# Small products run in halves, and the late modulation moved into the second scan and the output projection

## The chip, the core and the metric

The kernel runs on one core of a Trainium2 chip. The time is the device time of one execution in microseconds. Its engines are TensorE (matrix products; PE in the profile, PEld for its weight loads), VectorE (DVE), ScalarE (ACT), GpSimd (POOL) and SyncE (SP), whose queue issues all transfers. Each engine has a fixed list of instructions and runs it in order.

## The reference

One layer of a hybrid diffusion backbone: 512 latent tokens (`x`) and 256 context tokens, width 1024, all in float32.

```python
mod = silu(c) @ w_ada + b_ada                      # six vectors of 1024: sh1 sc1 gt1 sh2 sc2 gt2
h  = rms_norm(x, g_norm1) * (1 + sc1) + sh1        # hc likewise for the context
aq, ak, av, dq, dk, dv, dz, da, db, ga, gd = split_cols(h @ w_in)
y_attn = window_ctx_attention(...)                 # 8 query heads of 64, 2 key heads
o, _, _ = bidir_delta(q, k, v, g, beta, s_cf, s_cb) # gated delta rule, both directions, chunks of 64
y = sigmoid(ga) * (y_attn @ w_br_attn) + sigmoid(gd) * (merge_norm(o, dz) @ w_br_dn)
x1 = x + gt1 * (y @ w_out)
out = x1 + gt2 * (square(relu(modulate(rms_norm(x1, g_norm2), sc2, sh2) @ w_mlp1)) @ w_mlp2)
```

In the delta rule each chunk of 64 tokens and each of 8 heads needs the product of its keys with each other (`kk`), a triangular solve with it, and the product of queries and keys (`intra`). A scan over 4 context chunks and then over 8 latent chunks carries a 64x64 state for each head and direction.

## The kernel before, in words

**Large products.** All weights come in tiles of 128x1024 (512 KB, 256 KB for the branch projections). `wload` loads one into a ring of four slots (`wr`), ScalarE makes a rounded high part of it (L261) and VectorE the rest (L262). `mm3` and `gate_tiles` multiply with three products of 128x128 by 512 for each of eight slices, so a whole tile is 24 large products in one PSUM bank.

**Small products.** `half_products` (L690) makes, for four chunks at a time, the key products (source `kT`) or the query products (source `qT`) in blocks of 32: 128 products of 64x32 by 32, each of which is two matmul instructions in the profile, so 256 a call. It is called three times in `chunk_mats` (L702), once for each group of four chunks, and twice before the second scan (L1173). `combine` (L783) joins the inverses of the two halves of a chunk: a loop of 64 products of 32x32 (L791, L792), a copy of their result by ScalarE (L793), and a second loop of 64 (L800, L801). It is called once in the attention stage and twice between the scans (L1160).

**The order of the work.** The Python code writes the work of several generators in turn. `weave` takes the next piece of the generator that is least far on; the matrices of the delta rule (`mats`, 16 pieces) are woven with the attention inputs (`attn_in`, taken 32 times). `run_fill(n)` puts n large products from a filler (the attention branch projection, then gate tiles) between other work: `FILL[1]` = 28 before each `combine`, `FILL[2]` = 36 before each `half_products` of the queries, and 8, 7, 3 by turns in the three parts of a scan step. From this the framework's scheduler makes each engine's list, and may move pieces that don't depend on each other; TensorE's list was read for the counts below.

**The scan.** `chain_step` (L1037) is one chunk in one direction: products with the state (L1051), VectorE forms the residual (L1055, L1056), products with the inverse (L1063), VectorE scales (L1069) and ScalarE copies, products for the new state (L1082) and the output (L1100), VectorE makes the new state (L1093) and adds the output (L1105 or L1108). `steps` runs the two directions side by side and yields three times a step, 24 times in the eight latent steps.

**The late modulation.** `late_mod` (L999) computes the four modulation vectors that are needed late, in 4 groups of 8 steps: gt1, sh2, sc2, gt2. A step loads 512 KB of `w_ada` into a slot of the same ring `wr` (L1003) and reduces it on VectorE (L1005). `run_late(n)` takes n of the first 24 steps; the last 8 run in the MLP. gt1 is used in `residual` (L1268) by way of L1255, sc2 by way of L1283 (`mA`) and sh2 in the second norm (L277). `LATE` = 6, 3, 0 takes 6 before each `combine`, 3 before each `half_products` of the queries, none in the scan, and the rest behind it (L1201).

**The output projection** (L1275) is five tiles of 24 large products, each followed by `residual`, and three more tiles in halves of the tokens; then the second norm and the MLP.

Of the kernel before, what the change touches and what calls it, by code (L numbers as in the profile page):

```python
# [18 lines left out]
FILL = 144, 28, 36, (8, 7, 3)  # L19
# [6 lines left out]
ADVE = (4, 6)  # L26
ATT = 32
NHALF = 3
LATE = 6, 3, 0
NPL = ()  # L30
WEARLY = 0
ND1 = 3
# [10 lines left out]
HC = CH // 2  # L43
# [53 lines left out]
def tile_layer(ctx: ExitStack, tc: tile.TileContext, I: dict, out: bass.AP, dbg=None):  # L97
# [167 lines left out]
    def mm3(acc, w, xs, start=True, stop=True, ks=None):  # L265
        ks = list(range(len(xs))) if ks is None else ks
        n = len(ks)
        for i, k in enumerate(ks):
            xhi, xlo = xs[i]
            PE.matmul(acc, w[0][:, k, :], xhi, start=(start and i == 0), stop=False)  # L270
            PE.matmul(acc, w[0][:, k, :], xlo, start=False, stop=False)  # L271
            PE.matmul(acc, w[1][:, k, :], xhi, start=False, stop=(stop and i == n - 1))  # L272
# [286 lines left out]
    def weave(*work):  # L559

        done = [0] * len(work)
        while True:
            left = [(d / n, i) for i, (d, (_, n)) in enumerate(zip(done, work)) if d < n]
            if not left:
                break
            i = min(left)[1]
            next(work[i][0], None)
            done[i] += 1
# [65 lines left out]
    kT = [alloc(TOK, True) for _ in range(4)]  # L634
# [55 lines left out]
    def half_products(D_, O_, gi, src):  # L690

        for i in range(16):
            c, q = gi * 4 + i // 4, i % 4
            for x, dst in enumerate((D_, O_)):
                for h in range(2):
                    for a in range(2):
                        r = slice(64 * a, 64 * a + 64)
                        o, o2 = col(c) + HC * h, col(c) + HC * (h ^ x)
                        PE.matmul(dst[quad(a, h), i * HC:(i + 1) * HC], kT[q][r, o:o + HC], src[q][r, o2:o2 + HC],
                                  start=True, stop=True)  # L700

    def chunk_mats(gi):  # L702
        ms = slice(gi * 16, gi * 16 + 16)
        kD, kO = bank(), bank()
        half_products(kD, kO, gi, kT)
        yield
        dO = bank()
        for d in range(2):
            mg, mb = alloc(1024), alloc(512)
            row = lambda m_: m_[:, d, :].unsqueeze(1).broadcast_to([P, 16, HC])  # L710
            G.tensor_tensor(v3(mb.ap), row(nmask), bc(btok[:, d, ms], HC), op=ALU.mult)
            dp = bank()
            for x in range(2):
                gx = mg[:, x * 512:x * 512 + 512]
                V.tensor_tensor(v3(r32(gx)), row(mi), bc(gsp[:, x, d, ms], HC), op=ALU.mult)
                PE.matmul(dp.ap, trr[:, d, :], r32(gx), start=(x == 0), stop=(x == 1))
                PE.matmul(dO.ap, trr[:, 2 + d, :], r32(gx), start=(d == x == 0), stop=(d == x == 1))
            mg.free()
            if gi == 0:
                eb = alloc(512)  # L720
                e, na = eb.ap, neg[0][:, d * 512:d * 512 + 512]
            else:
                o = (gi - 1) * 512
                e, na = ED[d][:, o:o + 512], neg[1 + d][:, o:o + 512]
            act(e, dp.ap, AF.Exp)
            dp.free()
            V.tensor_tensor(e, e, mb.ap, op=ALU.mult)
            mb.free()
            V.tensor_tensor(na, e, kD.ap, op=ALU.mult)
            if gi == 0:  # L730
                eb.free()
            yield
        eb = alloc(512) if gi == 0 else None
        e = eb.ap if gi == 0 else EO[:, (gi - 1) * 512:gi * 512]
        act(e, dO.ap, AF.Exp)
        V.tensor_tensor(v3(e), v3(e), bc(tbO[:, ms], HC), op=ALU.mult)
        V.tensor_tensor(NTO[gi].ap, e, kO.ap, op=ALU.mult)
        for b in (kD, kO, dO, eb):
            if b:
                b.free()  # L740
        yield
# [38 lines left out]

        V.transpose(dst.rearrange("p m i -> p i m"), X3[g].rearrange("p r s -> p s r") if swap else X3[g])

    def combine(nto, XTf, XRf, XTb, XRb, XAf, XAb, inplace):  # L783

        Y, Ys = bank(), alloc(512)
        nt = v3(nto.ap)
        for i in range(16):
            o = slice(i * HC, (i + 1) * HC)
            for a in range(2):
                lo, hi = quad(a, 0), quad(a, 1)  # L790
                PE.matmul(Y[hi, o], nt[lo, i], XRf[lo, i], start=True, stop=True)  # L791
                PE.matmul(Y[lo, o], nt[hi, i], XRb[hi, i], start=True, stop=True)  # L792
        A.activation(Ys.ap, Y.ap, AF.Copy)  # L793
        Y.free()
        XO = bank()
        for i in range(16):
            o = slice(i * HC, (i + 1) * HC)
            for a in range(2):
                lo, hi = quad(a, 0), quad(a, 1)
                PE.matmul(XO[lo, o], Ys[hi, o], XTf[hi, i], start=True, stop=True)  # L800
                PE.matmul(XO[hi, o], Ys[lo, o], XTb[lo, i], start=True, stop=True)  # L801
        Ys.free()
        xo = v3(XO.ap)
        if not inplace:
            A.activation(XAf[:, :, :HC], XTf, AF.Copy)
            A.activation(XAb[:, :, :HC], XTb, AF.Copy)
        for a in range(2):
            lo, hi = quad(a, 0), quad(a, 1)
            A.activation(XAf[hi, :, HC:], XTf[hi], AF.Copy)
            A.activation(XAb[hi, :, HC:], XTb[hi], AF.Copy)  # L810
            A.activation(XAf[lo, :, HC:], xo[lo], AF.Copy)
            A.activation(XAb[hi, :, :HC], xo[hi], AF.Copy)
            G.memset(XAf[hi, :, :HC], 0.0)
            G.memset(XAb[lo, :, HC:], 0.0)
        XO.free()

# [16 lines left out]
    qT = []  # L833
# [8 lines left out]
    def mats():  # L842
        for q in range(4):
            l2n(kT[q].ap, 1.0, ((0, SEQ), (SEQ, TOK)), epsc)
            yield
        for gi in range(3):
            yield from chunk_mats(gi)
# [5 lines left out]
        yield from v_attn()  # L853

    att = attn_in()
    weave((mats(), 16), (att, ATT))
    tri_.free()
    trr_.free()
    lowm = alloc(1024)
# [160 lines left out]
    def run_late(n):  # L1020
        for _ in range(n):
            if late_n[0] < 24:
                late_n[0] += 1
                next(late)

    def run_fill(n):
        for _ in range(n):
            next(fill, None)
# [126 lines left out]
    for g in range(2):  # L1155
        ms = slice(16 * g, 16 * g + 16)
        f, b = xa[0][:, ms], xa[1][:, ms]
        run_fill(FILL[1])
        run_late(LATE[0])
        combine(NTO[1 + g], f[:, :, :HC], xr3[0][:, ms], b[:, :, :HC], xr3[1][:, ms], f, b, True)  # L1160
        NTO[1 + g].free()
    for b in xr:
        b.free()
# [3 lines left out]
    for g in range(2):  # L1167
        ms = slice(16 * g, 16 * g + 16)
        es = slice(512 * g, 512 * g + 512)
        run_fill(FILL[2])  # L1170
        run_late(LATE[1])
        qD, qO = bank(), bank()
        half_products(qD, qO, 1 + g, qT)  # L1173
        for d in range(2):
            V.tensor_tensor(ia[d][:, ms, :HC], v3(ED[d][:, es]), v3(qD.ap), op=ALU.mult)
        V.tensor_tensor(EO[:, es], EO[:, es], qO.ap, op=ALU.mult)
        qD.free()
        qO.free()
        eo = v3(EO[:, es])
        for a in range(2):  # L1180
            lo, hi = quad(a, 0), quad(a, 1)
            for d in range(2):
                A.activation(ia[d][hi, ms, HC:], ia[d][hi, ms, :HC], AF.Copy)
            A.activation(ia[0][lo, ms, HC:], eo[lo], AF.Copy)
            A.activation(ia[1][hi, ms, :HC], eo[hi], AF.Copy)
            G.memset(ia[0][hi, ms, :HC], 0.0)
            G.memset(ia[1][lo, ms, HC:], 0.0)
# [6 lines left out]
    ot = ot_.ap.rearrange("p (c q v) -> p c q v", c=NCL, q=4)  # L1194
    for n, _ in enumerate(steps(range(NCC, NC_))):
        run_fill(FILL[3][n % 3])
        if n % 3 == 2:
            run_late(LATE[2])
    for _ in fill:
        pass  # L1200
    run_late(24)  # L1201
    for b in kT + qT + KTM[1:] + VTM[1:] + XA[1] + IA + zb + Sb[0] + Sb[1]:
        b.free()

# [60 lines left out]
    def residual(ct, acc, cols):  # L1265

        x = xn_[ct][:, cols]
        V.scalar_tensor_tensor(x, acc.ap[:, cols], gt1h[:, ct:ct + 1], x, op0=ALU.mult, op1=ALU.add)  # L1268
        sq = ssq if ct == 0 else alloc(512)
        A.activation(sq[:, cols], x, AF.Square)  # L1270
        if ct:
            V.tensor_tensor(ssq[:, cols], ssq[:, cols], sq[:, cols], op=ALU.add)
            sq.free()

    for ct in range(8 - NHALF):  # L1275
        w = wnext()
        acc = bank()
        mm3(acc.ap, w, ys)
        residual(ct, acc, slice(0, 512))
        acc.free()  # L1280
    rx = alloc(512)
    mA = small([P, 8], "mA2", bufs=1)
    V.scalar_tensor_tensor(mA, modT[:, 2], 1.0, g2, op0=ALU.add, op1=ALU.mult)  # L1283
# [202 lines left out]
```

## Time and profile before

| | us |
|---|---|
| median of 3 runs | 958.29 (957.17 to 960.55) |
| the profiled execution | 959.2 |
| its span, first to last instruction | 957.4 |

| engine | busy, us | share | instructions |
|---|---|---|---|
| TensorE, matmuls | 917.7 | 96% | 7684 |
| TensorE, weight loads | 737.1 | 77% | 7684 |
| VectorE | 597.9 | 62% | 1010 |
| ScalarE | 449.3 | 47% | 827 |

The mean granted clock of TensorE over the span was 0.986. The page cuts the span into 40 slices of 23.9 us; a digit is the busy share in tenths, and PEclk is the granted clock in the same way. A group of instructions is named by its line in the kernel, its engine and its operation. A wait names the engine and line that ended it; "issue" stands for idle time that no other engine or transfer ended. TensorE busy does not mean TensorE at full speed: at a lowered clock it is busy as well. The stages, by the starts of their instructions: delta matrices about 105 to 155 us, first scan to about 372, `combine` and query products 372 to 431, second scan 431 to 512, branch and output projections 520 to 600, MLP to the end.

### The profile page before, as it was taken

How to read it: one execution, taken by the hardware profiler on the slowest of the kernel's cores; microseconds unless marked ns; L12 is line 12 of the kernel's file. 1: busy time of each engine (PE TensorE's matmuls, PEld its weight loads, DVE VectorE, ACT ScalarE, POOL GpSimd, SP SyncE). 2: the span in 40 equal slices, each digit the busy share in tenths (PEclk: the TensorE clock that was granted, in tenths of full speed). 3: DMA queues.
4: the chain of work that ended last, by engine and by line, in shares of the span. 5: the costliest groups of instructions: out<-in, count | busy, mean ns of one | idle time of the engine just before them, and what ended most of it. 6: DMA issues, size and time to landing. Idle time of an engine off the chain costs nothing. (4 is left out here: it accounts for less than half of the span.)

```text
span 957.4 us, 18072 instructions
## 1 busy us (share of the span) xinstructions
PE 917.7 (96%) x7684; PEld 737.1 (77%) x7684; DVE 597.9 (62%) x1010; ACT 449.3 (47%) x827; POOL 36.4 (4%) x45
## 2 busy tenths in 40 slices
PE   7999989989999999869999999999999999999998
PEld 3578767876877677658887889988888888888886
DVE  0876688997788899745567665982365225423511
ACT  6456745337667887337555433561154115313400
POOL 0000221000000000100011000000000000000000
PEclk9999999999999999888999999999999999999999
DMA  9742012110000133850114544382164214322101
GB/s 354 250 167 67 23 47 66 48 64 24 12 21 25 38 107 111 295 192 25 46 61 129 185 134 154 119 272 72 35 212 134 82 66 130 113 66 71 62 33 55
DMA packets 29889, 99.77 MB, mean 104 GB/s; under 512 B 3696, under 2 KB 4208, under 8 KB 29808
## 3 DMA queue, kind: packets, MB, share of 16 engines
q1 hardware_dynamic: 29808, 98.62, 31.4%
q8 instruction: 60, 0.98, 0.4%
q14 instruction: 21, 0.17, 0.1%
HBM read 96.51 MB, written 2.10 MB: 103 GB/s over the span
## 5 line engine op out<-in xcount | busy, mean ns | idle before, releaser
L271 PE MATMUL banks<-m,m 128*128 128x512 f32 (+1 forms) x568 | 213.4, 378 | 0.0
L272 PE MATMUL banks<-m,m 128*128 128x512 f32 (+1 forms) x568 | 212.5, 377 | 0.0
L270 PE MATMUL banks<-m,m 128*128 128x512 f32 (+1 forms) x568 | 210.5, 379 | 1.7 <-ACT m L276 1.7
L261 ACT ACTIVATE m<-wr 128x1024 fp32r<-128x1024 f32 x66 | 69.9, 1059 | 150.3 <-PE banks L271 78.1
L270 PEld LDWEIGHTS banks<-m,m 128*128 128x128 f32 x568 | 105.5, 188 | 23.7 <-issue 1.9
L271 PEld LDWEIGHTS banks<-m,m 128*128 128x128 f32 x568 | 106.3, 188 | 21.3 <-DVE m L198 0.9
L272 PEld LDWEIGHTS banks<-m,m 128*128 128x128 f32 x568 | 106.4, 188 | 19.9
L262 DVE TENSOR_TENSOR m<-wr,m 128x1024 fp32r<-128x1024 f32 x66 | 80.6, 1224 | 63.9 <-PE banks L271 34.2
L270 PE MATMUL banks<-m,wh 128*128 128x512 f32 (+1 forms) x328 | 119.7, 365 | 0.0
L271 PE MATMUL banks<-m,wh 128*128 128x512 f32 (+1 forms) x328 | 116.4, 355 | 0.0
L272 PE MATMUL banks<-m,wl 128*128 128x512 f32 (+1 forms) x328 | 116.1, 355 | 0.1
L940 PE MATMUL banks<-m,wh 128*128 128x512 f32 x320 | 108.1, 413 | 0.0
L1367 DVE SCALAR_TENSOR_TENSOR m<-banks,modT,m 128x512 f32<-128x512 f32 x32 | 24.0, 750 | 104.0 <-PE banks L272 104.0
L261 ACT ACTIVATE wh<-wr 128x1024 fp32r<-128x1024 f32 (+1 forms) x61 | 57.7, 946 | 54.2 <-PE banks L940 24.4
L262 DVE TENSOR_TENSOR wl<-wr,wh 128x1024 fp32r<-128x1024 f32 (+1 forms) x61 | 65.8, 1079 | 20.8 <-ACT wh L261 20.7
L940 PEld LDWEIGHTS banks<-m,wh 128*128 128x128 f32 x320 | 62.1, 197 | 17.1 <-issue 4.1
L940 PE MATMUL banks<-m,wl 128*128 128x512 f32 x160 | 66.9, 418 | 4.3 <-issue 4.3
L272 PEld LDWEIGHTS banks<-m,wl 128*128 128x128 f32 x328 | 61.8, 189 | 9.3 <-DVE wl L262 0.6
L270 PEld LDWEIGHTS banks<-m,wh 128*128 128x128 f32 x328 | 61.9, 189 | 8.9 <-ACT m L276 0.4
L271 PEld LDWEIGHTS banks<-m,wh 128*128 128x128 f32 x328 | 62.0, 189 | 8.4 <-issue 0.5
L181 ACT ACTIVATE m<-m 128x512 fp32r<-128x512 f32 (+1 forms) x56 | 35.0, 630 | 47.4 <-DVE m L1350 19.8
L182 DVE TENSOR_TENSOR m<-m,m 128x512 fp32r<-128x512 f32 (+1 forms) x56 | 38.2, 689 | 20.9 <-ACT m L181 20.4
(232 smaller groups left out, 1325.8 us busy)
## 6 DMA issues: line engine op xcount, KB each, us to landing
wr<-in_wm SPq DMA_DIRECT2D x64, 512.0 KB, 3.5
wr<-in_win SPq DMA_DIRECT2D x39, 512.0 KB, 3.6
wa<-in_wada SPq DMA_DIRECT2D x32, 512.0 KB, 4.3
m<-in_wada SPq DMA_DIRECT2D x16, 512.0 KB, 10.1
m<-in_xT SPq DMA_DIRECT2D x8, 512.0 KB, 6.7
wr<-in_wbr SPq DMA_DIRECT2D x16, 256.0 KB, 2.7
wr<-in_wout SPq DMA_DIRECT2D x8, 512.0 KB, 3.6
out<-m SPq DMA_DIRECT2D x8, 256.0 KB, 2.0
```

What stands on the lines that cost most here:

```text
L181: A.activation(r32(hi), src, AF.Copy)
L182: (eng or V).tensor_tensor(r32(lo), src, hi, op=ALU.subtract)
L261: A.activation(r32(hi), raw, AF.Copy)
L262: V.tensor_tensor(r32(lo), raw, hi, op=ALU.subtract)
L270: PE.matmul(acc, w[0][:, k, :], xhi, start=(start and i == 0), stop=False)
L271: PE.matmul(acc, w[0][:, k, :], xlo, start=False, stop=False)
L272: PE.matmul(acc, w[1][:, k, :], xhi, start=False, stop=(stop and i == n - 1))
L940: PE.matmul(acc.ap, w[x][:, k, :], hx[k][y], start=(k == p == 0), stop=(k == KT - 1 and p == 2))
L1367: V.scalar_tensor_tensor(xn_[ct], acc.ap, modT[:, 3, ct:ct + 1], xn_[ct], op0=ALU.mult, op1=ALU.add)
```

## The change

1. `half_products` becomes a generator that pauses after 8 of its 16 rounds. In `chunk_mats` the pause yields twice to `weave` (`HPAUSE` = 2), and `mats` counts 22 pieces instead of 16. Before the second scan, 12 of the 36 large products that stood ahead of the call (`FPAUSE`) are put into the pause.
2. `combine` gets a function that runs between its two loops; between the scans it runs 12 of the 28 large products that stood ahead of the call (`CPAUSE`). The `combine` in the attention stage is as before.
3. `LATE` is now 1: a late step in the second and the third part of each scan step (16 in all), none before `combine` and `half_products`, and two behind the product of each tile of the output projection until 24 are done (8 in all). The call that took the rest behind the scan now stands behind the output projection and finds none left.

```diff
-LATE = 6, 3, 0
+LATE = 1
+HPAUSE = 2
+FPAUSE, CPAUSE = 12, 12
@@ half_products
         for i in range(16):
+            if i == 8:
+                yield
             c, q = gi * 4 + i // 4, i % 4
@@ chunk_mats
-        half_products(kD, kO, gi, kT)
+        for _ in half_products(kD, kO, gi, kT):
+            for _ in range(HPAUSE):
+                yield
         yield
@@ combine
-    def combine(nto, XTf, XRf, XTb, XRb, XAf, XAb, inplace):
+    def combine(nto, XTf, XRf, XTb, XRb, XAf, XAb, inplace, between=lambda: None):
...
         A.activation(Ys.ap, Y.ap, AF.Copy)
         Y.free()
+        between()
         XO = bank()
@@
-    weave((mats(), 16), (att, ATT))
+    weave((mats(), 16 + 3 * HPAUSE), (att, ATT))
@@ between the scans
-        run_fill(FILL[1])
-        run_late(LATE[0])
-        combine(NTO[1 + g], f[:, :, :HC], xr3[0][:, ms], b[:, :, :HC], xr3[1][:, ms], f, b, True)
+        run_fill(FILL[1] - CPAUSE)
+        combine(NTO[1 + g], f[:, :, :HC], xr3[0][:, ms], b[:, :, :HC], xr3[1][:, ms], f, b, True, lambda: run_fill(CPAUSE))
...
-        run_fill(FILL[2])
-        run_late(LATE[1])
+        run_fill(FILL[2] - FPAUSE)
         qD, qO = bank(), bank()
-        half_products(qD, qO, 1 + g, qT)
+        for _ in half_products(qD, qO, 1 + g, qT):
+            run_fill(FPAUSE)
@@ second scan
         run_fill(FILL[3][n % 3])
-        if n % 3 == 2:
-            run_late(LATE[2])
+        if n % 3:
+            run_late(LATE)
     for _ in fill:
         pass
-    run_late(24)
@@ output projection
         mm3(acc.ap, w, ys)
+        run_late(2)
         residual(ct, acc, slice(0, 512))
         acc.free()
+    run_late(24)
```

## The prediction

> **What bounds the kernel now.** I read the page first, then TensorE's waits, then a table of stretches cut at the stalls.
>
> ```profile
> span 957.4 us, 18072 instructions
> PE 917.7 (96%) x7684; PEld 737.1 (77%) x7684; DVE 597.9 (62%) x1010; ACT 449.3 (47%) x827; POOL 36.4 (4%) x45
> PEclk9999999999999999888999999999999999999999
> q8 instruction: 60, 0.98, 0.4%
> ```
>
> TensorE is busy 96% of the span, so only its idle time and its slow clock can be won. The clock dips in one place, slices 16 to 18.
>
> ```profile
> PE banks L699 <- issue: 6.5, 3, 4.0
> PE banks L800 <- issue: 4.4, 3, 2.1
> PE banks L940 <- issue: 4.3, 1, 4.3
> PE banks L699 <- DVE m L729: 2.7, 1, 2.7
> PE banks L1063 <- DVE m L1056: 0.9, 1, 0.9
> ```
>
> These are TensorE's waits (us, times, longest). 15.2 us are "issue": no engine or transfer released them, and all lie in or just behind the small products of `half_products` (L699) and `combine` (L800). The next table has the stalls and the stretches around them: length, busy time and count of each engine, then granted clock, DMA share, GB/s.
>
> ```profile
> 107.20:108.47 1.27, 1.27 (x151) 1.15 (x139) 0.51 (x1) 1.27 (x4) 0.00 (x0) 1.00 0.06 13
> 108.47:110.69 2.22, 0.00 (x0) 0.00 (x0) 2.22 (x6) 2.17 (x5) 0.93 (x1) 1.00 0.00 0
> 379.48:382.24 2.76, 2.52 (x144) 1.84 (x131) 2.21 (x5) 1.98 (x3) 0.00 (x0) 1.00 0.84 267
> 382.24:384.33 2.09, 0.00 (x1) 0.00 (x1) 1.98 (x4) 0.00 (x0) 0.00 (x0) 1.00 0.92 308
> 384.33:392.60 8.27, 8.27 (x134) 6.64 (x136) 4.91 (x9) 4.02 (x6) 1.04 (x2) 0.79 0.91 319
> 392.60:395.00 2.40, 2.40 (x143) 1.82 (x132) 2.40 (x4) 0.60 (x1) 0.00 (x0) 1.00 0.75 242
> 395.00:397.11 2.11, 0.01 (x2) 0.00 (x0) 2.11 (x5) 0.00 (x0) 0.00 (x0) 1.00 0.77 262
> 397.11:408.32 11.21, 11.21 (x264) 9.18 (x265) 7.85 (x14) 4.01 (x6) 3.10 (x6) 0.85 0.85 288
> 408.32:409.53 1.21, 1.21 (x144) 1.17 (x131) 0.74 (x2) 0.00 (x0) 0.00 (x0) 1.00 0.78 288
> 409.53:413.79 4.26, 0.01 (x1) 0.11 (x2) 0.68 (x1) 0.00 (x0) 0.00 (x0) 0.76 0.79 281
> 413.79:425.17 11.38, 11.38 (x135) 8.99 (x137) 8.25 (x14) 7.91 (x12) 1.04 (x2) 0.79 0.58 186
> 425.17:426.38 1.21, 1.21 (x144) 1.10 (x131) 0.12 (x1) 0.00 (x0) 0.00 (x0) 1.00 0.44 81
> 426.38:430.39 4.01, 0.00 (x1) 0.00 (x1) 0.00 (x0) 0.00 (x0) 0.00 (x0) 0.80 0.32 111
> 430.39:437.00 6.61, 6.61 (x108) 5.86 (x107) 3.40 (x7) 5.04 (x9) 1.03 (x2) 0.60 0.02 5
> 680.00:700.00 20.00, 20.00 (x89) 16.38 (x88) 10.92 (x11) 6.55 (x7) 0.00 (x0) 1.00 0.43 140
> ```
>
> Between one stall and the next lie whole multiples of 128 matmuls with their 128 weight loads (the counts hold a few that straddle an edge). The instruction queue moves 0.98 MB in 60 packets, and 2 x 7684 TensorE instructions over 60 are 256 a packet. So TensorE waits for its own code: each stall sits where a packet of 256 instructions ends and the next has not arrived. The time from entering a packet to having the next is the stretch plus the stall: 1.27 + 2.22 = 3.5 us with DMA idle, and 4.85, 4.5, 5.5 and 5.2 us in the later four, where the DMA share was 0.3 to 0.9. A small product costs 1.21 us/131 = 9.2 ns, a large one 20/88 = 0.227 us. A packet of 128 small products lasts 1.2 us and so starves; one of large ones lasts 29 us.
>
> [...]
>
> Each stall is followed by a lowered clock. Outside the stalls the loss is length times (1 - clock): 8.27 x 0.21 + 11.21 x 0.15 + 11.38 x 0.21 + 6.61 x 0.40 = 8.45 us. The stalls of that stage are 2.09 + 2.11 + 4.26 + 4.01 = 12.47 us.
>
> **The change, part by part.**
>
> *Halves in `combine` and in the second `half_products`.* The fill products of `run_fill` are not new, 12 are moved into each run. Counted in the written instruction order, the starving packets of before hold 124 small products and 4 large (the 1st, 2nd), 122 and 6 behind one of 128 (the 3rd), and 128 (the 4th). With the change all the tight ones hold 116 small and 12 large, 1.07 + 2.72 = 3.8 us, but for one of 122 and 6: 2.5 us. Against 3.5 us that leaves nothing and 1.0 us; against 5.2 us, 1.4 us four times and 2.7 us once. The 18 late loads have left the stage, but one weight load per 24 large products stays and the first late loads of the scan come in early. I take the quiet row, which fits better, with a meeting now and then: 2.0 us in all (ends 1.0 and 8.3). Stalls: -10.5 us. No stall then is much over 1 us, so I keep half of one lowered stretch (8.45/4 = 2.1), 1.0 us: -7.4 us.
>
> The moved 12 no longer stand ahead of the first `combine`, which needs the last transposes of L781.
>
> ```profile
> 372.28 4.44 DVE L781 STREAM_TRANSPOSE m<-m 128x1024 f32<-128x1024 f32 x2
> 378.87 0.21 PE L791 MATMUL banks<-m,m 32*32 32x32 f32 x1
> ```
>
> L791 would come at 378.87 - 2.72 = 376.15, and L781 ends at 376.72: +0.6 us. Within `combine` the pause covers the copy L793 that loop two waits for.
>
> *Halves in `chunk_mats`.* Here the scheduler decides. In the written order group 0 runs 48, 80 and 128 small products with 4 and then 15 others between, and its stall of 2.2 us goes; but its products now stand 12 large ones earlier (up to 2.7 us) and may wait for the last normalised `kT`. Group 1 still runs 256 in one go, now with a packet of 128 small whole inside: 3.5 - 1.2 = 2.3 us of new stall, where before it was 6.5 - 2.22 - 4.01 = 0.3. Group 2 still waits for L729. VectorE is busy 48.98 of the 60 us here, so TensorE's gain is only partly handed on.
>
> ```profile
> 100.00:160.00 60.00, 53.90 (x954) 41.53 (x952) 48.98 (x68) 31.61 (x53) 14.13 (x9) 0.94 0.18 54
> ```
>
> The ends: all idle time of the stage but the wait for L729 and all of the clock's 60 x 0.06 = 3.6 us won (-6), or a second stall with its slow clock (+4). I take -1.
>
> *Late modulation.* Before, 12 late steps stand in the `combine` stage, 6 in the second `half_products` and 6 behind the scan; now 16 stand in the second scan and 8 in the output projection. A step is one 512 KB load (SP's queue, slots shared with the weights) and 1.22 + 0.08 us on VectorE.
>
> ```profile
> L1005 DVE SCALAR_TENSOR_TENSOR m<-wa,m x32: 1206/1221/1502, 378.3 to 631.9; 128x1024 f32<-128x1024 f32 x32
> DVE m L1005 <- DMA wa<-in_wada: 11.4, 8, 4.0
> wa<-in_wada SPq DMA_DIRECT2D x32, 512.0 KB, 4.3
> 437.00:512.00 75.00, 74.11 (x1320) 60.23 (x1320) 46.62 (x99) 45.10 (x154) 5.24 (x6) 1.00 0.21 67
> 447.71 0.89 DVE L1069 TENSOR_TENSOR m<-banks,eg 128x256 f32<-128x256 f32 x2 [1.47 <-PE banks L1063]
> 450.68 0.42 DVE L1093 TENSOR_TENSOR m<-m,banks 128x256 f32<-128x256 f32 x1 [2.07 <-PE banks L1082]
> 453.97 0.42 DVE L1055 TENSOR_TENSOR m<-banks,eg 128x256 f32<-128x256 f32 x1 [1.55 <-PE banks L1051]
> 455.36 0.42 DVE L1056 SCALAR_TENSOR_TENSOR m<-m,m 128x256 f32<-128x256 f32 x1
> 456.82 1.15 PE L1063 MATMUL banks<-m,m 64*64 64x64 f32 x32
> ```
>
> A scan step lasts about 75/8 = 9.4 us and leaves VectorE three gaps, 1.47, 2.07 and 1.55 us. A late step of 1.30 us fits into one; two, or one behind a weight split (L262, 1.22 us), don't. The link that follows then has about 1.0 us in hand (L1056 ends 455.78, L1063 starts 456.82). In the written order about half of the 16 stand alone in a gap; one link has three of them around L1055 and L1056 (3.9 - 1.55 - 1.0 = 1.3 us late), two have late step and weight split together (about 0.4 each). I take +2.0 us. The ends: 0, and 16 x 1.30 = 20.8 us if none is covered. A late step that waits for its load holds the scan's operations behind it on VectorE; by the written order slots are freed half a step to a step ahead of use, and a load lands in 4.3 us, so I add nothing. In the scan a packet lasts 75/(1320/128) = 7.3 us, over the 5.5 us of the worst fetch, so the added loads start no stall there. Behind the scan, L1063's 0.9 us wait, where late steps stood, goes: -0.9.
>
> In the output projection 8 steps add 10.4 us to a VectorE that is busy 17.04 of 30 us, and `residual` and the weight splits behind them have a product of 24 x 0.227 = 5.5 us each to hide in; three loads a product instead of one are 1.5 MB in 5.5 us, 286 GB/s, less than the 319 above. L1283, which needs the last of them, now comes behind the fourth product, more than two products (11 us) ahead of its use. Zero; without that cover up to 8 x 1.30 = 10 us.
>
> ```profile
> 560.00:590.00 30.00, 30.00 (x157) 25.64 (x156) 17.04 (x20) 11.79 (x15) 0.00 (x0) 1.00 0.41 126
> ```
>
> **Sum.** -10.5 - 7.4 + 0.6 - 1.0 + 2.0 - 0.9 = -17.2 us. The profiled execution took 959.2 us (span 957.4 and 1.8 around it), 0.9 over the median of 958.3; so 942.0 by its own time, 941.1 by the median. I say 942.
>
> **The rivals.**
> 1. *The fetch is slow by itself*, not by the loads beside it. For it: the stall at 426.38 lasted 4.01 us while the DMA share fell to 0.32. Against: 3.5 us at 108.47. Then the stalls keep 8.3 us and the clock about half, 4.2: 12.47 - 8.3 = 4.2 won, 4.2 of the clock, and the other terms' +0.7: -7.7, 951 us.
> 2. *The other terms turn out well*: the first stage gives 4 and the late steps cost nothing: -17.2 - 3.0 - 2.0, 937 us. For it: three gaps a step. Against: group 1.
> 3. *Slower*: the late steps stand on the scan's path. It decides from 17.2 + 2.0 = 19.2 us, 1.20 us for each of 16, which is nearly all of 20.8: 942 + 18.8 = 961 us. For it: 11.4 us of waits for loads before. Against: the gaps.
> 4. *The change doesn't do what it says*: the stalls come from something else in the small products and stay, with the clock. Then only +0.6 + 2.0 - 0.9 remain: 961 us. Against: the count of 128.
>
> [...]
>
> **How the numbers follow.** The forecast 0.55, rival 1 0.17, rival 2 0.18, rival 3 0.05, rival 4 0.05. The range must leave out no more than 0.2: 934 to 953 takes in the first, second and the forecast with its 2 to 6 us of doubt in the scan and the first stage. About 0.3% (2.9 us) is what a measurement of this kernel can tell from no change. Faster 0.91; rivals 3 and 4 end about there or above, same 0.03, slower 0.06.
>
> **What would show it.** Right: TensorE's "issue" waits between the first `combine` and the scan fall from 12.5 us to under 3, the clock's dips in slices 16 to 18 are gone, and a new issue stall of about 2 us stands in group 1 of `chunk_mats`. The scan shows 16 of L1005, with TensorE waits for L1056 or L1093 of about 2 us. Wrong: waits of L1005 for its loads inside the scan, TensorE waiting for weights in the output projection, or stalls at the same 128-matmul borders that are as long as before.

## The result, and the profile after

The changed kernel takes 948.24 us, median of 4 runs (947.43 to 951.25), against 959.42 (957.17 to 963.79) for the kernel before on the same chip. The ratio is 0.9884, with a 95% interval of 0.984 to 0.9927: faster by about 11 us, where 17 were forecast. The profiled execution took 947.43 us. All line numbers of the changed kernel are a little higher: `half_products` is L703 (before L699), the two loops of `combine` are L797/L798 and L807/L808 (L791/L792, L800/L801), the fill products L947 (L940), the scan L1058, L1070, L1089, L1107 (L1051, L1063, L1082, L1100), a late step L1012 (L1005), `residual` L1273 (L1268). Some experiments shift these by a line or three.

The page of the changed kernel: busy times and the clock in 40 slices.

```profile
PE 915.7 (97%) x7684; PEld 733.2 (78%) x7684; DVE 598.2 (63%) x1010; ACT 449.4 (48%) x827; POOL 37.6 (4%) x45
PEclk9999979999999999999999999999999999999999
```

The clock's dip in slices 16 to 18 is gone, and a new one stands in slice 5 (the count starts at 0; 118 to 142 us), in the first stage. The same 60 packets of code are fetched. Of TensorE's waits in the changed kernel (us, times, longest) these bear on the change:

```profile
PE banks L397 <- ACT m L394: 4.3, 2, 2.4
PE banks L722 <- issue: 1.6, 1, 1.6
PE banks L703 <- issue: 1.4, 1, 1.4
PE banks L272 <- DVE m L1273: 1.3, 1, 1.3
PE banks L1070 <- DVE m L1063: 1.0, 2, 0.9
PE banks L1058 <- DVE m L1100: 0.8, 1, 0.8
```

The "issue" waits of over 1 us have gone from 15.2 us in three rows to 3.0 in two, and both that are left lie in the first stage (L722 is in `chunk_mats`). The wait for L397 has grown from 2.2 us. New are waits for VectorE: L1100 in the scan, L1273 in the output projection (the one for L1063 was 0.9 us before).

The stage that the change is about, from the last transposes of the first scan to the first output product of the second, as one stretch (length, busy time and count of TensorE, granted clock, DMA share, GB/s), in the kernel before:

```profile
372.28:440.60 68.32, 55.62 (x1283) 0.85 0.56 187
```

and in the changed kernel:

```profile
374.21:424.50 50.29, 49.17 (x1281) 1.00 0.32 98
```

With the same matmuls, TensorE's idle time fell from 12.70 to 1.12 us, and its busy time from 55.62 us at a mean clock of 0.85 to 49.17 at full clock.

To say where the 12.1 us of span come from I cut the span at three events that each kernel has once: the start of the last pair of transposes of the first scan (VectorE, L781/L787), and the first and the last start of the scan's output products (L1100/L1107). These are the rows of the kernel before (the transposes stand in the prediction):

```profile
L1100 PE MATMUL banks<-m,m x256: 218/218/267, 440.6 to 511.3; 64*64 64x64 f32 x128
```

and of the changed kernel:

```profile
374.21 4.43 DVE L787 STREAM_TRANSPOSE m<-m 128x1024 f32<-128x1024 f32 x2
```

```profile
L1107 PE MATMUL banks<-m,m x256: 218/218/267, 424.5 to 497.8; 64*64 64x64 f32 x128
```

The same two rows and the span of every other kernel give this table (us; the experiments follow below). A is the first stage up to the transposes, B the stage between the scans, C the second scan, D all that comes after it.

| kernel | A | B | C | D | span |
|---|---|---|---|---|---|
| before | 372.3 | 68.3 | 70.7 | 446.1 | 957.4 |
| after | 374.2 | 50.3 | 73.3 | 447.5 | 945.3 |
| e7_change_again | 374.1 | 49.8 | 73.5 | 447.4 | 944.8 |
| e1_first_whole | 374.3 | 50.8 | 74.3 | 448.5 | 947.9 |
| e2_halves_only | 372.5 | 59.1 | 71.6 | 446.0 | 949.2 |
| e3_late_only | 374.2 | 56.4 | 72.7 | 449.7 | 953.0 |
| e4_pause6 | 374.9 | 56.2 | 74.0 | 448.1 | 953.2 |
| e5_late_12_12 | 374.3 | 56.9 | 71.1 | 447.9 | 950.2 |
| e6_late_8_16 | 373.3 | 59.1 | 72.6 | 446.0 | 951.0 |
| e9_no_late | 375.2 | 49.0 | 69.9 | 446.1 | 940.2 |
| e10_gate_loop | 375.7 | 49.8 | 73.5 | 447.6 | 946.6 |
| e11_behind_scan | 374.5 | 50.9 | 73.5 | 446.1 | 945.0 |
| e12_eight | 375.7 | 49.2 | 69.9 | 445.5 | 940.3 |
| e13_phase | 375.2 | 50.2 | 74.7 | 446.8 | 946.9 |

After against before: A +1.9, B -18.0, C +2.6, D +1.4, which is -12.1. The stage between the scans won a little more than was forecast (-17.3); the three other stretches gave back 5.9 us where +0.1 was forecast. The change profiled once more (e7) repeats each stretch within 0.5 us.

### The profile page after: what moved, and what is told of

Same layout as the page of the kernel before. It is cut to its first block, busy times and chain, and to the rows that moved or that the text cites. A ratio compares the mean times of both kernels' runs of the same rounds, so it can differ in the third digit from the quotient of the medians.

```text
span 945.3 us, 18083 instructions
## 1 busy us (share of the span) xinstructions
PE 915.7 (97%) x7684; PEld 733.2 (78%) x7684; DVE 598.2 (63%) x1010; ACT 449.4 (48%) x827; POOL 37.6 (4%) x45
## 4 chain that ended last, share of the span: by engine, by line
PE 79%; DVE 10%; ACT 4%; DMA 4%; issue 2%; POOL 1%; SPq 0%; POOLq 0%; DVEq 0%; ACTq 0%
PE banks L272 17%; PE banks L273 16%; PE banks L274 16%; PE banks L947 10%; DMA wa<-in_wada 3%; PE banks L992 2%; PE banks L223 2%; DVE wl L264 2%; PE banks L530 1%; PE banks L703 1%; PE banks L1058 1%; ACT m L147 1%; PE banks L536 1%; PE banks L1070 1%; PE banks L1089 1%
## 5 line engine op out<-in xcount | busy, mean ns | idle before, releaser
L274 PE MATMUL banks<-m,m 128*128 128x512 f32 (+1 forms) x568 | 213.1, 377 | 0.0
L263 ACT ACTIVATE m<-wr 128x1024 fp32r<-128x1024 f32 x66 | 69.8, 1060 | 152.1 <-PE banks L273 92.0
L264 DVE TENSOR_TENSOR m<-wr,m 128x1024 fp32r<-128x1024 f32 x66 | 80.6, 1224 | 75.3 <-PE banks L273 38.7
L274 PEld LDWEIGHTS banks<-m,m 128*128 128x128 f32 x568 | 106.6, 188 | 19.7
L274 PE MATMUL banks<-m,wl 128*128 128x512 f32 (+1 forms) x328 | 116.9, 357 | 0.5 <-DVE wl L264 0.4
L947 PE MATMUL banks<-m,wh 128*128 128x512 f32 x320 | 105.0, 401 | 0.0
L264 DVE TENSOR_TENSOR wl<-wr,wh 128x1024 fp32r<-128x1024 f32 (+1 forms) x61 | 65.9, 1080 | 33.9 <-ACT wh L263 33.5
L263 ACT ACTIVATE wh<-wr 128x1024 fp32r<-128x1024 f32 (+1 forms) x61 | 57.7, 946 | 33.1 <-PE banks L273 18.3
L274 PEld LDWEIGHTS banks<-m,wl 128*128 128x128 f32 x328 | 62.3, 190 | 9.6 <-DVE wl L264 1.2
L947 PEld LDWEIGHTS banks<-m,wh 128*128 128x128 f32 x320 | 59.4, 188 | 12.1
L947 PE MATMUL banks<-m,wl 128*128 128x512 f32 x160 | 65.2, 408 | 0.3 <-DVE wl L264 0.3
```

The costliest lines, as they stand in the source:

```text
L263: A.activation(r32(hi), raw, AF.Copy)
L264: V.tensor_tensor(r32(lo), raw, hi, op=ALU.subtract)
L947: PE.matmul(acc.ap, w[x][:, k, :], hx[k][y], start=(k == p == 0), stop=(k == KT - 1 and p == 2))
```

## The experiments

All edits are against the changed kernel.

**The runs of `chunk_mats` left whole** (e1). Is the slower first stage the work of the halves in `chunk_mats`?

```diff
-HPAUSE = 2
+HPAUSE = 0
```

> The change without its first part: the calls in chunk_mats run whole again, as in the kernel before; the pauses of 12 and the new places of the late steps stay. Theory (the halves in chunk_mats cost what they were to win, because TensorE's order there lost the cover of a wait for ScalarE and a packet stays whole): the first stage gives back its 1.9 us, so the profiled span goes from 945.3 to about 943.4, with the stalls of the kernel before (2.2 and 0.3 us of issue) at 108 and 124 us. Rival (the 1.9 us come from elsewhere, or are paid back later, since VectorE bounds the stretch from 160 to 220 us): span 945 or more.

Measured: 947.55 us (946.32 to 950.02), ratio 0.9906 (0.9885 to 0.9927) to the kernel before, no different from the change. The first stage still ended 2.0 us late. Its waits were those of the kernel before (2.4 us of "issue" and 2.5 us for L735, the L729 of before), but the clock was lowered once more, at 208.6 us, behind a wait for L579. The wait and the stretch of this kernel:

```profile
PE banks L489 <- DVE m L579: 2.4, 1, 2.4
```

```profile
208.60:212.00 3.40, 3.40 (x12) 0.50 0.24 47
```

The kernel before has the same wait (L487 for L577), and full clock behind it:

```profile
PE banks L487 <- DVE m L577: 2.4, 1, 2.4
```

```profile
160.00:215.00 55.00, 51.24 (x287) 1.00 0.16 49
```

So the halves of `chunk_mats` are not shown to cost anything, nor to win anything. Column A of the eight kernels that run this part whole (e1 to e6, e9, e12) goes from 372.5 to 375.7 us with the same code there as before; the five with halves lie between 374.1 and 375.7. So the kernel before, at 372.3, seems to be a favourable execution of this stage.

**Each half of the change alone.** First the halves with the late steps unmoved (e2): `LATE` back to 6, 3, 0 at its old places (ahead of `combine`, ahead of `half_products`, in the scan, and the rest behind it), the late steps of the output projection gone.

```diff
-LATE = 1
-HPAUSE = 2
+LATE = 6, 3, 0
+HPAUSE = 0
...
+        run_late(LATE[0])
...
+        run_late(LATE[1])
...
-        if n % 3:
-            run_late(LATE)
+        if n % 3 == 2:
+            run_late(LATE[2])
+    run_late(24)
...
-        run_late(2)
...
-    run_late(24)
```

> The pauses of 12 alone: chunk_mats whole and the late steps in their old places. Theory (each stall is the time to fetch a packet less the time that the packet before it lasts; a fetch takes 3.5 us alone and 4.5 to 5.5 beside the late loads): packets of 3.8 us against fetches of 4.5 to 5.5 leave stalls of 0.7 to 1.7 us four times and one of 2 to 3, 5 us in all instead of 12.5, and some of the slow clock; span about 948. Rival (12 products cover the fetch whatever the loads do): no stall, span about 940 since the scan keeps its room. Rival (the loads alone make the stalls): 12 us of stalls as before, span near 957.

Measured: 952.8 us (950.18 to 957.47), ratio 0.9967 (0.9945 to 0.9989). B fell by 9.2 of 18.0 us. TensorE's waits of this kernel between 370 and 436 us:

```profile
PE banks L947 <- ACT wh L263: 2.6, 1, 2.6
PE banks L807 <- DVE m L1012: 1.8, 1, 1.8
PE banks L807 <- ACT m L799: 1.1, 1, 1.1
```

and VectorE's in the same window:

```profile
DVE m L1012 <- DMA wa<-in_wada: 5.9, 6, 3.5
```

and ScalarE's:

```profile
ACT wh L263 <- DMA wr<-in_win: 8.1, 2, 4.1
ACT m L799 <- DVE m L1012: 3.2, 2, 1.8
```

No "issue" wait is left, though the DMA share of the stage is no lower than before (0.64 against 0.56). But the late steps reach TensorE in two ways, 5.5 us in all. They wait 5.9 us for their loads and hold VectorE, and through it ScalarE's copy L799 and the second loop of `combine` (L807: 2.9 us). And the weight loads, which share their queue and slots, come late: between 370 and 412 us they took 4.4 to 6.6 us to land (median of the kernel before 3.6), ScalarE's split L263 waited for them, and TensorE for the split (L947: 2.6 us). One slow stretch follows:

```profile
400.70:407.50 6.80, 6.17 (x137) 0.50 0.72 257
```

The stalls for code were the first in line; with them gone, the late steps and the loads beside them were next. (Whether 12 products alone would hide the fetch beside these loads can't be read here: the new waits gave the fetch time too.)

Then the late steps moved and the runs left whole (e3):

```diff
-HPAUSE = 2
-FPAUSE, CPAUSE = 12, 12
+HPAUSE = 0
+FPAUSE, CPAUSE = 0, 0
```

> The late steps in their new places alone: no run of small products is paused. Theory (fetch less packet): packets of 2.0, 2.0, 2.5 and 2.5 us against 3.5 leave stalls of about 1.5, 1.5, 1.0 and 1.0, so 5 us instead of 12.5, and with the slow clock behind some of them; with +4 us in the scan and the output projection the span is about 952. Rival (the loads alone make the stalls): none left between 375 and 431 us, span about 943, as fast as the whole change without its first part.

Measured: 953.62 us (952.1 to 955.09), ratio 0.9963 (0.9949 to 0.9978); B fell by 11.9. TensorE's waits in the same window:

```profile
PE banks L703 <- issue: 2.2, 1, 2.2
PE banks L947 <- issue: 1.9, 1, 1.9
PE banks L807 <- issue: 1.5, 2, 1.2
```

and two instructions of its timeline:

```profile
403.83 2.36 PE L703 MATMUL banks<-m,m 64*32 64x32 f32 x256
408.11 0.39 PE L947 MATMUL banks<-m,wl 128*128 128x512 f32 x1 [1.93 <-issue]
```

Without the late loads 5.6 us of "issue" remain of 12.5. A run of 256 small products, two packets, takes 2.4 us, and then TensorE stands for 1.93. If the second packet was entered half way, at 405.0, the next had arrived 3.1 us later, at a DMA share of 0.02. I call this time a fetch; the traces show where it ends, and its start is my estimate. With loads beside it the same took 4.5 to 5.5 us before; and counted back by 128 products in the same way, the 2.2 us stall of e3 ended a fetch of about 5 us at a DMA share of 0.84. So beside loads a fetch took longer here, but the stalls are there without the late loads.

**Half the pause** (e4). Six large products in each pause instead of twelve.

```diff
-HPAUSE = 2
-FPAUSE, CPAUSE = 12, 12
+HPAUSE = 0
+FPAUSE, CPAUSE = 6, 6
```

> As the first of these runs, with pauses of 6 large products instead of 12. Theory (fetch less packet): packets of 122 small and 6 large products last 2.5 us, 1.3 us less than with 12, so stalls of about 1.0 us four or five times, 4 to 5 us of issue where the pauses of 12 have none, and little slow clock: span 4 to 6 us over the first of these runs. [...]

Measured: 954.09 us (951.12 to 955.46), ratio 0.9966 (0.9947 to 0.9985). TensorE's waits in the same window:

```profile
PE banks L807 <- issue: 2.7, 2, 2.1
PE banks L703 <- issue: 1.7, 1, 1.7
PE banks L947 <- issue: 0.7, 1, 0.7
```

5.1 us of "issue", hardly less than with no pause, and B is the same (56.2 to 56.4). With twelve (e1) B is 50.8 and two waits of 0.7 and 0.6 us are left. Six large products last 6 x 0.227 = 1.4 us, too little beside a fetch of about 3.1 us (e3) or more; twelve last 2.7. (The longest stall here ended a fetch of about 5 us, again counted back by 128 products, at a DMA share of 0.34 only: the share alone doesn't settle how long a fetch takes.)

**The change again** (e7), unedited, beside the next kernels.

> The whole change once more. Theory (the first stage is slower because of its instruction order): at 150 us the products stand 1 us or more behind the kernel before again, with waits for ScalarE of about 2.4 us at 119 us and for issue at 125 and 143 us. [...]

Measured: 946.84 us (945.71 to 947.03), ratio 0.9871 (0.9849 to 0.9893). TensorE's long waits are those of the change (L397 4.3 us, "issue" 1.5 and 1.3).

**Late steps spread in other ways.** Half of them (3 at a time) back ahead of `combine` and `half_products`, twelve in the scan, none behind it (e5):

```diff
-HPAUSE = 2
+HPAUSE = 0
...
+        run_late(3)
...
+        run_late(3)
...
-        if n % 3:
+        if n % 3 == 1 or n % 6 == 2:
...
-        run_late(2)
```

> The first of these runs (chunk_mats whole, pauses of 12) with the late steps in other places: three before each combine and each half_products of the queries, 12 in the scan (the second part of each step, the third part of every other), none in the output projection. Theory (each place takes only as many late steps as VectorE has gaps for: in the run with the old places the 18 between the scans blocked VectorE at the head of its queue while their loads were under way, and 16 in the scan and 8 in the output projection cost some 7 us): 12 beside the pauses cost 1 to 3 us there, the scan 1 to 2 instead of 4.6, the output projection nothing: span 942 to 944, 3 us or more under the whole change. Rival (between the scans any late step costs what it saves, by slower fetches or a blocked VectorE): span 946 or more.

Measured: 950.95 us (949.71 to 953.15), ratio 0.9916 (0.9885 to 0.9947). And eight (2 at a time) there with sixteen in the scan as in the change (e6):

```diff
-HPAUSE = 2
+HPAUSE = 0
...
+        run_late(2)
...
+        run_late(2)
...
-        run_late(2)
```

> The same with two late steps before each combine and half_products, the 16 of the change in the scan and none in the output projection. Theory: the output projection gives back its 1.5 to 2.5 us and the scan keeps its cost, with 0 to 1 us for the 8 steps beside the pauses: span 943 to 945. Rival (the seam behind the output projection costs the same without the moved steps, since the steps of the last group stand there as well): no gain against the first of these runs.

Measured: 954.4 us (953.05 to 954.7), ratio 0.9956 (0.9931 to 0.9981). Both miss what I had expected. B rose from the 50.8 of e1 to 56.9 and 59.1, though only 12 and 8 of the 24 late steps stand there. TensorE's waits of e5 and of e6 in the same window:

```profile
PE banks L703 <- ACT m L147: 2.2, 1, 2.2
PE banks L947 <- issue: 2.1, 1, 2.1
```

```profile
PE banks L703 <- ACT m L147: 8.0, 2, 7.4
```

and, of e6, ScalarE's longest wait there, which ended at 399.7 us:

```profile
ACT m L1098 <- DVE m L1012: 9.5, 1, 9.5
```

ScalarE stood 9.5 us behind a late step on VectorE, whose own load was 3.2 us late, and the copy L147 that frees a bank for `half_products` stood behind it on ScalarE. In this stage even two late steps in each place reach TensorE; in these runs they belong out of it altogether.

**What the late steps cost where they are now** (e9). All 24 left out.

```diff
-HPAUSE = 2
+HPAUSE = 0
...
+    V.memset(modT, 1.0)
...
-    late = (x for grp in range(4) for x in late_mod(grp))
-    late_n = [0]
+    late = (x for grp in (3,) for x in late_mod(grp))
+    late_n = [24]
```

> As the first of these runs, with the 24 late steps of the first three groups left out (gt1, sh2 and sc2 are set to one, so the output is not the layer's). It prices them. Theory: the scan and the output projection cost nothing over the kernel before, so the gain of 16.4 us that stands at the first step of the scan is there at the end: span about 940. Rival (the scan's 4.6 us are not from the late steps but from the scan meeting a faster TensorE): span 944 or more.

Measured: 941.94 us in one run, against 947.55 for e1, the same kernel with the late steps. C is 69.9 us and D 446.1, the D of the kernel before. Its row:

```profile
L1108 PE MATMUL banks<-m,m x256: 218/218/267, 424.2 to 494.1; 64*64 64x64 f32 x128
```

So the late steps cost 73.3 - 69.9 = 3.4 us in the scan and 1.4 behind it, by the profile of the change. (C of the other kernels with sixteen in the scan lies between 72.6 and 74.7; e1, which differs from e9 in the late steps alone, has 74.3, and a D of 448.5.) The kernel before had lost 70.7 - 69.9 = 0.8 us to its own late steps at the scan's end.

**One late step a scan step** (e12), eight in all, the other sixteen left out:

```diff
-HPAUSE = 2
+HPAUSE = 0
...
+    V.memset(modT, 1.0)
...
-    late = (x for grp in range(4) for x in late_mod(grp))
+    late = (x for grp in (0, 3) for x in late_mod(grp))
...
-            if late_n[0] < 24:
+            if late_n[0] < 8:
...
-        if n % 3:
+        if n % 3 == 1:
```

> As the first of these runs, with only eight late steps before the MLP, one in the second part of each scan step; 16 are left out (sh2 and sc2 are set to one, so the output is not the layer's). Theory (a late step alone in a gap of VectorE is free; what cost 3.8 us was two in one gap or one beside a weight split): the scan ends within 1 us of the run without any late step. Rival (every step costs its share, 0.24 us): 1.9 us later.

Measured: 942.11 us in one run. Its scan row:

```profile
L1108 PE MATMUL banks<-m,m x256: 217/218/267, 424.9 to 494.8; 64*64 64x64 f32 x128
```

C is 69.9 us, as with none: eight late steps are free in the scan, sixteen cost the 3.4 us. (In the profiles seven of the eight and 13 of the sixteen start within C, the others ahead of it. Two of the seven fell into one scan step, at 470.95 and 472.43 us, and were free as well.) In this kernel no late step waited for its load. In the change four do (VectorE's wait, 424 to 500 us):

```profile
DVE m L1012 <- DMA wa<-in_wada: 3.4, 4, 1.3
```

and this is how late steps reach TensorE in the change. VectorE first:

```profile
473.13 1.22 DVE L1012 SCALAR_TENSOR_TENSOR m<-wa,m 128x1024 f32<-128x1024 f32 x1 [1.25 <-DMA wa<-in_wada]
...
486.80 1.22 DVE L1012 SCALAR_TENSOR_TENSOR m<-wa,m 128x1024 f32<-128x1024 f32 x1
489.08 0.42 DVE L1119 TENSOR_REDUCE oss<-m 128x4 f32<-128x256 f32 x1 [1.06 <-ACT m L1118]
...
490.08 1.22 DVE L1012 SCALAR_TENSOR_TENSOR m<-wa,m 128x1024 f32<-128x1024 f32 x1
```

then GpSimd's add in the change, and the same add (there L1118) in e12:

```profile
487.02 1.58 POOL L1117 TENSOR_TENSOR m<-m,m 128x256 f32<-128x256 f32 x1 [8.36 <-DVE m L1115]
```

```profile
486.82 0.72 POOL L1118 TENSOR_TENSOR m<-m,m 128x256 f32<-128x256 f32 x1 [0.20 <-DVE m L1116]
```

and TensorE in the change:

```profile
475.17 0.68 PE L1089 MATMUL banks<-m,m 64*64 64x64 f32 x16 [0.61 <-ACT m L1080]
489.88 1.15 PE L1058 MATMUL banks<-m,m 64*64 64x64 f32 x32 [0.81 <-DVE m L1100]
493.94 1.15 PE L1070 MATMUL banks<-m,m 64*64 64x64 f32 x32 [0.85 <-DVE m L1063]
```

At 473 the late step comes 1.25 us late to VectorE; L1076 waits behind it, ScalarE's copy behind that, and TensorE stands 0.61. At the scan's end the two late steps have their data, and reach TensorE by way of GpSimd. In the last four scan steps GpSimd adds the output (L1117), ScalarE squares it (L1118) and VectorE reduces the square (L1119). Beside the late step the add takes 1.58 us, and beside the next one 1.59; in e9 and e12 none of them takes over 0.74. So VectorE stands idle 1.06 and then 1.07 us in front of L1119, and L1100 (once) and L1063 (once) come late behind it: 0.81 and 0.85. With an add of 0.73 us VectorE would have gone on 0.85 us sooner, which is about each of the two waits (an estimate from these rows). The kernels agree: e9 and e12 have no slow add and no wait of TensorE in the scan, the kernel before has one (1.59 us, at 503.85) and one wait (0.9), the change two and two. No run moves the add alone, so this chain is read from the order of the events. All TensorE waits in the scan come to 2.6 us of the 3.4.

**Another phase of the sixteen** (e13), with the other eight behind the scan:

```diff
-        if n % 3:
+        if n % 3 != 2:
...
+    run_late(24)
...
-        run_late(2)
```

> As the run with the eight steps behind the scan, but the late steps of the scan stand in the first and second part of each step instead of the second and third. Theory (late steps are free as long as each has a gap of VectorE to itself): in the written order fewer of them share a link, so the scan costs 2 to 3 us instead of 3.8, span 943 to 944. Rival (16 steps beside the weight splits fill the gaps whatever their phase): scan as before, span 945.

Measured: 947.81 us (946.21 to 949.81), ratio 0.9896 (0.9859 to 0.9932). C is 74.7, though the waits of late steps for loads fell to 2.0 us: other links of the scan wait now. TensorE's largest wait in the scan is that for L1100, 1.7 us in three waits, and three of GpSimd's adds are slow (1.70, 1.58 and 1.65 us), one beside a weight split on VectorE and two beside late steps. This other phase gains nothing. How much of the 3.4 us is due to late loads, to the slow adds or to VectorE's own load, these runs don't separate in full.

**Where the eight of the output projection go.** Half of them in the gate tiles that follow the scan (e10):

```diff
-    for _ in gate_tiles(gates[12 + NGD:]):
-        pass
+    for n, _ in enumerate(gate_tiles(gates[12 + NGD:])):
+        if n % 18 == 0:
+            run_late(1)
...
-        run_late(2)
+        run_late(1)
```

> The whole change, with four of the eight late steps of the output projection moved ahead into the three gate tiles behind the scan, and one instead of two behind each of the first four tiles of the output projection. Theory (the 1.5 us at the seam behind the output projection are from its 16 late loads standing ahead of weights, residual and the steps of the last group): 0.5 to 1 us come back, span 944. Rival (what was late at the seam is the step of the last group, which stays): span 945 as the change.

Measured: 947.97 us (946.66 to 949.68), ratio 0.9906 (0.987 to 0.9942): no gain, D 447.6. And all eight directly behind the scan (e11), where the kernel before had its rest:

```diff
+    run_late(24)
...
-        run_late(2)
```

> The whole change, with all eight late steps of the output projection at the old place behind the scan. Theory: the seam behind the output projection is as in the kernel before (1.5 us back), but the scheduler takes the steps into the end of the scan, where L1217 and the transposes wait behind them on VectorE (8 x 1.3 = 10 us there, covered by 72 large products or 16 us): 0 to 1 us lost there, span 943 to 945. Rival (L1217 starts the chain to the output projection and is not covered): 3 us or more lost there, span 947 or more.

Measured: 946.27 us (944.33 to 946.89), ratio 0.9885 (0.9855 to 0.9914); D is 446.1, so the 1.4 us behind the scan are gone. The total can't be told from that of the change. The place in the change with the longest wait, VectorE and then TensorE:

```profile
579.46 1.22 DVE L1012 SCALAR_TENSOR_TENSOR m<-wa,m 128x1024 f32<-128x1024 f32 x1 [0.82 <-DMA wa<-in_wada]
580.61 0.48 DVE L1273 SCALAR_TENSOR_TENSOR m<-banks,gt1h,m 128x256 f32<-128x256 f32 x1
```

```profile
581.15 0.39 PE L272 MATMUL banks<-m,wh 128*128 128x256 f32 x1 [1.34 <-DVE m L1273]
```

The late step at 579.46 is none of the eight, which have all started by 564.23. It is the first of the last group of eight, which every kernel runs from here into the MLP. The scheduler set it ahead of `residual` L1273; in e9, e11 and the kernel before it comes behind all but one of the `residual` operations. Column D goes with this: 447.4 us or more in the seven kernels where that step stands ahead (the change, e1, e3, e4, e5, e7, e10), 446.8 or less in the seven where it doesn't. e5 is among the first with none of the 24 in the output projection, and e10 with four.

No kernel here that computes the whole layer beats the change; it, e1 and e11 are level.

## Why the prediction was right or wrong

The sign, the range and the main cause were right; the forecast of 942 was 5.4 us too fast for the profiled execution. Of the signs named for being wrong two showed, both small: late steps waited 3.4 us for their loads inside the scan, and TensorE 0.4 us for a weight split in the output projection (L274 for L264). By the terms of its sum:

*Stalls -10.5, clock -7.4, L781 +0.6: right.* B fell by 18.0 against 17.3. The signs named for it are there: "issue" between the first `combine` and the scan went from 12.5 us to 0.3, and the dips are gone. The cause, a packet of 256 instructions that is used up before the next has come, held in e3 and e4: the stalls outlive the removal of the late loads (5.6 us of "issue" left in e3), a pause of 1.4 us does not help (5.1 us in e4), one of 2.7 us does (0.3 us in the change). That rules out rival 4. Rival 1, a fetch slow by itself, did not come: with DMA quiet a fetch took about 3.1 us in e3, and the 8.3 us of stalls that it kept are gone. The parts of the sum fit less well than the sum. TensorE's idle time fell by 11.6 us, more than 10.5, since hardly any of the 2.0 us kept for loads that meet a fetch was needed. Its busy time fell by 6.45 with all of the clock back, so the 8.45 us that I had put down to the clock were too many. And TensorE shows no wait for L787 (L781 before) at the first `combine`, so the +0.6 is not seen.

With 12 large products in the pause no stall over 0.7 us is left in this stage (e1); with none or 6 single stalls reach 2.2 and 2.1 us (e3, e4).

*Old lates behind the scan -0.9: right.* 70.7 against 69.9 us without any late step is 0.8.

*Scan +2.0: mis-sized, and its nearness is partly luck.* The sixteen late steps cost 3.4 us. Two steps failed. The first is "so I add nothing" for loads that come late inside the scan: four of them waited, 3.4 us on VectorE, and TensorE's wait of 0.61 us at 475.17 stands behind the longest. The second is that gaps were counted on VectorE alone. TensorE waited 1.7 us for L1063 and L1100 at the scan's end, where "about 2 us" was said; but not for three late steps around one link, which show no wait. The late steps there stand beside GpSimd's add, which then takes 1.6 us instead of 0.73, and the sum has no term for that. That a late step fits in a gap for nothing is what e12 shows.

*Halves in `chunk_mats` -1.0 (-6 to +4): wrong in sign in the profile, and not settled.* The stall of group 0 went and one of 1.37 us came in group 1, as argued (I had 2.3). The wait of group 2 for L729, which was to stay, went too. Two things were overlooked. A packet in group 2 held 125 small products and 3 large and starved too (1.65 us, L722). And with the first eight rounds moved ahead, nothing was left to run while ScalarE prepared the operand of L397:

```profile
121.11 1.12 PE L397 MATMUL banks<-m,c_bones 128*128 128x512 f32 x2 [2.45 <-ACT m L394]
126.66 1.41 PE L703 MATMUL banks<-m 64*32 64x32 f32 x89 [1.37 <-issue]
```

```profile
122.30:132.50 10.20, 8.52 (x267) 0.50 0.16 55
160.00:215.00 55.00, 51.69 (x279) 0.97 0.17 56
```

These rows are of the changed kernel, instructions and then two stretches. The clock is at half (0.50) for 10.2 us behind the wait of L397, which lasted 2.45 us, and once more behind 160 (55 x 0.03 = 1.7 us lost). The waits of "issue", L397 and the old L729 add up to 7.3 us here (4.3 + 1.6 + 1.4) against 2.5 + 2.7 + 2.2 = 7.4 before; the clock cost 5.1 + 1.7 = 6.8 us against 60 x 0.06 = 3.6. But e1, with its runs whole, meets such a stretch too, in another place, and ends as late. Nor was there much clock to win: e2 has a granted clock of 1.00 from 100 to 365 us and ends the stage at 372.5, the kernel before has 0.94 from 100 to 160 and ends it at 372.3. What this part of the change is worth lies within the 3 us by which that stage differs between kernels with the same code.

*Output projection 0: wrong, +1.4.* I had looked at the average, VectorE busy 17.04 of 30 us and 5.5 us of cover a product. But the cover fails at one place: where the tiles of 24 products give way to those in halves of the tokens, `residual` L1273 is waited for at once, and one late step with a late load stands in front of it (0.82 + 1.22 us). That step belongs to the last group, which the prediction did not look at; its place in VectorE's list changed with the order that the scheduler made. Where it comes behind (e9, e11) D is 446.1, as before.

Rival 3 named the right place for the loss (VectorE's chain in the scan) at a sixth of its price, 3.4 of up to 20.8 us. Rival 2, that the late steps cost nothing, is what e12 shows for eight of them; sixteen would have to go elsewhere.

## What to carry to other kernels

Where TensorE runs some 250 small products with little between them, look in its waits for "issue" at borders of 128 matmuls. Here they came to 12.5 us in one stage, read as TensorE waiting for its own code; a dozen large products (2.7 us) moved into the middle of each run left 0.3 us of them, while half a dozen (1.4 us) left 5.1. When such a stall goes, ask what stands right behind it: here the late steps, which had to leave the stage as well, so that each half of the change alone won 9 to 12 us of the stage (e2, e3) and both together 18. And don't cover side work by the average load of an engine, nor by the gaps of one engine alone: eight late steps in the scan were free (e12), sixteen cost 3.4 us, and half of that, 1.7 us of TensorE's waits, stands behind an add on GpSimd that took 1.6 us beside them instead of 0.73. In the output projection one late load (0.82 us) in front of a single urgent operation made the longest wait (1.34 us), and it belonged to a step that nobody had moved.

## What the runs showed of the hardware

An add of 128x256 on GpSimd took 0.72 to 0.74 us by itself in the scan, and 1.58 to 1.59 beside a late step on VectorE in the change.

Whether a short wait of TensorE is followed by a stretch at half clock is not settled by its length. The stretches at half clock that I saw last 3.4 us (e1, e3), 6.8 (e2) or 10.2 (the change). The wait for ScalarE at L395/L397 is an example. In e3 it was followed by one:

```profile
161.53 1.14 PE L397 MATMUL banks<-m,c_bones 128*128 128x512 f32 x1 [1.83 <-ACT m L394]
```

```profile
161.70:165.10 3.40, 3.40 (x8) 0.51 0.00 0
```

In the kernel before the same wait was as long, and the clock stayed full (the row 160 to 215 us above):

```profile
161.36 1.12 PE L395 MATMUL banks<-m,c_bones 128*128 128x512 f32 x2 [1.80 <-ACT m L392]
```

By the clock of 0.50 or 0.51 in these rows, a stretch of 3.4 us costs about 1.7 us of TensorE's work where nothing covers it (an estimate, 3.4 x 0.5). Single profiles of kernels with the same code differ by 3 us in one stage (372.5 to 375.7 in column A), and a gain below that is to be read from the waits and the medians, not from one span. What decides whether the clock falls is open.
